# Moving a matmul kernel's steady-state transposes off TensorE, onto ScalarE, GpSimd and VectorE

## The chip, the cores and the metric

One core of a Trainium2 chip. The metric is the device time of one execution in microseconds (us). All times below are medians of runs in the fast state; how a ratio is formed is said at the result.

## The reference

```python
def setup_inputs():
    batch, m, k, n = 16, 512, 1024, 768
    # x (16,512,1024), weight (1024,768), add_value (16,512,768): float32 normal; scale 0.1

def reference(x, weight, scale, add_value):
    return (scale * np.matmul(x, weight) + add_value).astype(np.float32)
```

The rows are cut into 64 tiles of 128. A tile needs 0.52 MB of x, 0.39 MB of added values and 0.39 MB of stores; with 3.15 MB of weights the kernel moves 87.03 MB.

## The kernel before

x is cast to bf16; two bf16 neighbours are then looked at as one fp32 word, so a 128x1024 tile turns as four 128x128 blocks of words. Of every five tiles in the middle of the kernel, three are turned by TensorE (into PSUM, the memory that it writes, and moved from there to SBUF, the memory that it reads, by ScalarE: the evacuation) and two by VectorE, in sixteen block transposes a pair. All transfers are issued by SyncE, strictly in the order of `STREAM`; x has 16 slots, the added values and outputs share 32 slots.

```python
STREAM = [   # (what, first tile, tiles): the order in which SyncE issues transfers
    ("x", 0, 3), ("w", 0, 2), ("w", 2, 2), ("w", 4, 2), ("x", 3, 1), ("w", 6, 2),
    ("a", 0, 3), ("x", 4, 4), ("a", 3, 5), ("x", 8, 4), ("x", 12, 4), ("a", 8, 8),
    ("x", 16, 8), ("a", 16, 8), ("x", 24, 8), ("a", 24, 8), ("o", 0, 8), ("x", 32, 8),
    # ... cut ...
    ("o", 48, 8), ("o", 56, 4), ("o", 60, 3), ("o", 63, 1),
]
PAIRS = [14, 19, 24, 29, 34, 39, 44, 49, 54, 59]     # tiles t0 and t0+1, turned by VectorE

def cast_pair(t0):                                   # vx has one buffer
    for i in range(2):
        nc.gpsimd.tensor_copy(vx[:, i, :], xs[:, (t0 + i) % X_SLOTS, :])
def turn_pair(t0, a):                                # called in four successive steps
    for b in range(0, P, 32):
        nc.vector.transpose(
            vt[b:b + 32, :, 32 * a:32 * a + 32], pairs[32 * a:32 * a + 32, :, b:b + 32])
def transpose(t, pieces=1):
    # ... cut: cast_to(t); pairs = the cast tile as fp32 words ...
    for c in range(KC):
        nc.tensor.transpose(tp[:, c, :], pairs[:, c * P:(c + 1) * P], identity)
    # ... cut: ScalarE copies tp into xt ...
def step():
    for j in range(KJ):                              # 8 x (512 + 256 columns)
        if j == KJ // 2:
            if t + 1 not in in_pair: transpose(t + 1)
            cast_to(min(t + AHEAD, done["x"] - 1))   # AHEAD = 6
            if t + 7 in PAIRS: cast_pair(t + 7)
        product(t, j, BOTH)
    finish(t, BOTH[0], 0, N)                         # VectorE: ao = scale * mm + ao
    for a in range(4):
        if t + 6 - a in PAIRS: turn_pair(t + 6 - a, a)
```

## Time and profile before

| | before |
|---|---|
| time, median of 3 | 210.93 us (210.76 to 211.62) |
| span of the profiled run | 209.1 us |
| TensorE busy | 193.2 us, 92% |
| VectorE, ScalarE, GpSimd busy | 138.2, 47.2, 63.3 us |
| DMA | 87.03 MB, 97.7% of the 16 engines' span |

The prediction shows the lines. Two columns of the view by stretches: the DMA share (the mean busy share of the 16 DMA engines; 1.00 means that they were busy all the time, and in short stretches the view can read a little more) and the GB/s beside it.

### The profile page before, as it was taken

The page shows a single profiled execution, that of the slowest core. Times are in us where ns is not written, and L with a number is a line of the kernel's source. Part 1 is how long each engine was busy: PE and PEld are TensorE (multiplying, and loading weights), DVE is VectorE, ACT ScalarE, POOL GpSimd, SP SyncE. Part 2 cuts the span into 40 slices and gives each one's busy share as a digit, 9 for nine tenths or more (in the row PEclk, how much of TensorE's full clock was granted, in tenths as well). Part 3 has the DMA queues.
Part 4 walks back from the last instruction along what each step waited for, and adds up shares of the span by engine and source line. Part 5 has one row for each costly group of instructions (what it writes and reads, how often), then busy time and mean ns, then how long its engine had stood idle before and what let it go on. Part 6 is the DMA issues. An engine that isn't in the chain of part 4 may idle for free.

```text
span 209.1 us, 2949 instructions
## 1 busy us (share of the span) xinstructions
PE 193.2 (92%) x1187; PEld 117.9 (56%) x1210; DVE 138.2 (66%) x239; ACT 47.2 (23%) x50; POOL 63.3 (30%) x69
## 2 busy tenths in 40 slices
PE   7599499999899999999999999998999999999980
PEld 2355265665566566665666665564665656666640
DVE  0535533219969959999686986839994996973330
ACT  2523123323112113023031121130130230310210
POOL 1310524820292090502902707202703029200000
PEclk9889999999999999999999999999999999999998
DMA  6999999999999999999999999999999999999984
GB/s 235 418 425 444 424 422 429 450 450 407 423 456 417 418 437 395 458 439 422 431 429 425 440 428 423 437 429 423 428 432 432 458 404 423 432 440 432 407 378 179
DMA packets 4909, 87.21 MB, mean 417 GB/s; under 512 B 544, under 2 KB 544, under 8 KB 1312
## 3 DMA queue, kind: packets, MB, share of 16 engines
q1 hardware_dynamic: 4896, 87.03, 97.7%
q8 instruction: 9, 0.15, 0.3%
q14 instruction: 4, 0.03, 0.0%
HBM read 61.87 MB, written 25.17 MB: 416 GB/s over the span
## 4 chain that ended last, share of the span: by engine, by line
DMA 56%; PE 27%; DVE 8%; POOL 3%; issue 1%; SPq 0%; POOLq 0%; DVEq 0%
DMA xs<-in_x_dram 28%; PE mm L167 25%; DMA out_dram<-ao 16%; DMA ao<-in_add_value_dram 8%; DVE vt L119 5%; DMA ao<-in_weight_dram 4%; POOL vx L108 3%; PE tp L145 3%; DVE ao L175 2%; POOL xb L135 1%; SPq L101 0%; SPq L247 0%; POOLq L108 0%; POOLq L135 0%; DVEq L175 0%
## 5 line engine op out<-in xcount | busy, mean ns | idle before, releaser
L167 PE MATMUL mm<-w_bf,xt 128*128 128x512 bf16 (+1 forms) x687 | 122.1, 327 | 1.5 <-DVE ao L203 0.4
L167 PEld LDWEIGHTS <-xt 128*128 128x128 bf16 x704 | 66.0, 98 | 48.1 <-ACT xt L151 10.9
L175 DVE SCALAR_TENSOR_TENSOR ao<-mm,ao 128x768 f32<-128x768 f32 (+2 forms) x62 | 58.2, 944 | 43.9 <-PE mm L167 24.4
L151 ACT COPY xt<-tp 128x1024 bf16<-128x1024 bf16 (+1 forms) x47 | 44.6, 959 | 147.2 <-PE tp L145 147.2
L119 DVE STREAM_TRANSPOSE vt<-vx 32x256 f32<-32x256 f32 x160 | 69.7, 435 | 8.4 <-POOL vx L108 6.0
L135 POOL CAST xb<-xs 128x1024 bf16<-128x1024 f32 x41 | 41.3, 1042 | 55.7 <-DMA xs<-in_x_dram 55.7
L167 PE MATMUL mm<-w_bf,vt 128*128 128x256 bf16 (+1 forms) x314 | 54.6, 325 | 1.7 <-DVE vt L119 1.4
L167 PEld LDWEIGHTS <-vt 128*128 128x128 bf16 x320 | 31.1, 98 | 21.4 <-DVE vt L119 2.1
L108 POOL CAST vx<-xs 128x1024 bf16<-128x1024 f32 x20 | 20.3, 1042 | 53.7 <-DVE vt L119 43.3
L145 PE MATMUL tp<-identity,xb 128*128 128x128 f32 x176 | 27.1, 277 | 5.4 <-POOL xb L135 3.0
L145 PEld LDWEIGHTS tp<-identity,xb 128*128 128x128 f32 x176 | 20.7, 142 | 11.8 <-POOL xb L135 3.4
L103 DVE CAST w_bf<-ao 128x768 bf16<-128x768 f32 x8 | 4.1, 556 | 3.9 <-DMA ao<-in_weight_dram 3.9
L131 DVE CAST xb<-xs 128x512 bf16<-128x512 f32 x3 | 1.9, 697 | 5.8 <-DMA xs<-in_x_dram 5.8
L93 PE MATMUL warm<-zeros 128*128 128x512 bf16 x10 | 4.4, 631 | 1.2 <-DVE zeros L81 1.2
L203 DVE TENSOR_SCALAR ao<-mm 128x768 f32<-128x768 f32 x2 | 1.8, 953 | 2.4 <-PE mm L167 2.4
L133 POOL CAST xb<-xs 128x512 bf16<-128x512 f32 x2 | 1.6, 836 | 5.7 <-DMA xs<-in_x_dram 5.7
L93 PEld LDWEIGHTS <-zeros 128*128 128x128 bf16 x10 | 1.3, 142 | 3.4 <-issue 2.2
L234 DVE TENSOR_TENSOR ao<-ao 128x768 f32<-128x768 f32 x3 | 2.7, 950 | 0.0
L133 ACT CAST xb<-xs 128x512 bf16<-128x512 f32 x1 | 0.6, 618 | 5.0 <-DMA xs<-in_x_dram 5.0
L133 ACT ACT_TABLE_LOAD x1 | 1.3, 1283 | 0.7 <-PEq L277 0.7
L81 DVE MEMSET zeros<- 128x256 uint32 x1 | 0.3, 272 | 0.9 <-PEq L277 0.9
L200 ACT ACTIVATE ao<-mm 128x768 f32<-128x768 f32 x1 | 0.8, 817 | 0.0
(6 smaller groups left out, 0.9 us busy)
## 6 DMA issues: line engine op xcount, KB each, us to landing
xs<-in_x_dram SPq DMA_DIRECT2D x6, 4096.0 KB, 27.1
ao<-in_add_value_dram SPq DMA_DIRECT2D x7, 3072.0 KB, 24.2
out_dram<-ao SPq DMA_DIRECT2D x7, 3072.0 KB, 31.2
xs<-in_x_dram SPq DMA_DIRECT2D x3, 2048.0 KB, 25.2
ao<-in_weight_dram SPq DMA_DIRECT2D x4, 768.0 KB, 9.8
ao<-in_add_value_dram SPq DMA_DIRECT2D x1, 1920.0 KB, 21.1
xs<-in_x_dram SPq DMA_DIRECT2D x1, 1536.0 KB, 6.2
out_dram<-ao SPq DMA_DIRECT2D x1, 1536.0 KB, 12.3
```

The source lines that it names most:

```text
L93: nc.tensor.matmul(warm[:, 0:CUT], zeros[:, 0:P], zeros, start=True, stop=True)
L103: nc.vector.tensor_copy(w_bf[:, j + i, :], ao[:, s + i, :])
L108: nc.gpsimd.tensor_copy(vx[:, i, :], xs[:, (t0 + i) % X_SLOTS, :])
L119: nc.vector.transpose(vt[b:b + 32, :, 32 * a:32 * a + 32], pairs[32 * a:32 * a + 32, :, b:b + 32])
L131: nc.vector.tensor_copy(xb[:, 0:K // 2], src[:, 0:K // 2])
L133: other(xb[:, K // 2:K], src[:, K // 2:K])
L135: nc.gpsimd.tensor_copy(xb, src)
L145: nc.tensor.transpose(tp[:, c, :], pairs[:, c * P:(c + 1) * P], identity)
L151: nc.scalar.copy(dst[:, c:c + q, :, :], src[:, c:c + q, :, :])
L167: nc.tensor.matmul(mm_tiles[t, cols[0]][:, n0:n1], lhs(t, j), w_bf[:, j, n0:n1], start=(j == 0), stop=(j == KJ - 1))
L175: nc.vector.scalar_tensor_tensor(a, mm_tiles[t, part][:, n0:n1], float(scale), a, op0=mybir.AluOpType.mult, op1=mybir.AluOpType.add)
L234: nc.vector.tensor_add(ao[:, t, :], ao[:, EARLY_AT + t, :], ao[:, t, :])
```

## The change

Its intent is to take the transposes of tiles 14 to 59 off TensorE. A pair of tiles is cast and at the same time moved between 32-partition quadrants by ScalarE or GpSimd (alternately), 16 small copies a pair; one VectorE transpose then turns all 32x32 blocks. The order of transfers is redone for it: x comes earlier, added values later, and the last stores are smaller. The warm-up matmuls go, and the PSUM evacuation of tiles 4 to 13 moves from ScalarE to VectorE.

```diff
-    ("a", 0, 3), ("x", 4, 4), ("a", 3, 5), ("x", 8, 4), ("x", 12, 4), ("a", 8, 8),
-    ("x", 16, 8), ("a", 16, 8), ("x", 24, 8), ("a", 24, 8), ("o", 0, 8), ("x", 32, 8),
-    ...
-    ("o", 48, 8), ("o", 56, 4), ("o", 60, 3), ("o", 63, 1),
+    ("a", 0, 3), ("x", 4, 4), ("a", 3, 1), ("a", 4, 4), ("x", 8, 4), ("x", 12, 4),
+    ("x", 16, 4), ("a", 8, 8), ("x", 20, 4), ("x", 24, 8), ("o", 0, 8), ("a", 16, 8),
+    ("x", 32, 8), ("a", 24, 8), ("a", 32, 8), ("x", 40, 8), ("o", 8, 8), ("x", 48, 8),
+    ("a", 40, 8), ("o", 16, 8), ("x", 56, 8), ("a", 48, 8), ("o", 24, 8), ("o", 32, 8),
+    ("a", 56, 8), ("o", 40, 8), ("o", 48, 8), ("o", 56, 4), ("o", 60, 1), ("o", 61, 1),
+    ("o", 62, 1), ("l", 63, 1), ("r", 63, 1),          # left and right part of tile 63
-PAIRS = [14, 19, 24, 29, 34, 39, 44, 49, 54, 59]
+MOVED_ACT = [14, 18, 22, 26, 30, 34, 38, 42, 46, 50, 54, 58]
+MOVED_POOL = [16, 20, 24, 28, 32, 36, 40, 44, 48, 52, 56]
-AHEAD = 6
+AHEAD = 4
-    for _ in range(WARM):                              # ten warm-up matmuls
-        nc.tensor.matmul(warm[:, 0:CUT], zeros[:, 0:P], zeros, start=True, stop=True)
+    def move_pair(t0, a):                              # steps t0-8 to t0-5, a = 0..3
+        for b in range(4):
+            move = nc.scalar.copy if act else nc.gpsimd.tensor_copy
+            move(moved[t0][32 * b:32 * b + 32, :, a, :], src[32 * a:32 * a + 32, :, b, :])
+    def turn_moved(t0):                                # step t0-4, after its final add
+        nc.vector.transpose(
+            xt.rearrange("p i c m -> p (i c m)"),
+            moved.pop(t0).bitcast(fp32).rearrange("p c a k -> p (c a k)"))
     (cut: pools, the layout of xt, the loops that call these)
+        evacuate = nc.scalar.copy if t <= EARLY or t > LAST_PAIR else nc.vector.tensor_copy
```

## The prediction

> **What bounds the kernel now.** I read the page first: engine shares, slices, queue shares, chain.
>
> ```profile
> span 209.1 us, 2949 instructions
> PE 193.2 (92%) x1187; PEld 117.9 (56%) x1210; DVE 138.2 (66%) x239; ACT 47.2 (23%) x50; POOL 63.3 (30%) x69
> DMA  6999999999999999999999999999999999999984
> q1 hardware_dynamic: 4896, 87.03, 97.7%
> DMA 56%; PE 27%; DVE 8%; POOL 3%; issue 1%; SPq 0%; POOLq 0%; DVEq 0%
> ```
>
> Two things look full: TensorE (92%) and the DMA engines (97.7%). The reader should see that the row of DMA digits has no hole. Then I asked for busy time by stretch, to see how full the DMA really is:
>
> ```profile
> 0.00:5.00 5.00, 3.81 (x9) 1.34 (x10) 0.27 (x1) 1.28 (x1) 0.70 (x6) 1.00 0.67 231
> 5.00:200.00 195.00, 186.46 (x1162) 115.03 (x1184) 135.85 (x235) 45.85 (x49) 62.62 (x63) 0.99 1.00 429
> 200.00:205.00 5.00, 2.94 (x18) 1.49 (x16) 2.08 (x3) 0.11 (x1) 0.00 (x0) 1.00 0.90 377
> 205.00:210.00 5.00, 0.00 (x0) 0.00 (x0) 0.00 (x0) 0.00 (x0) 0.00 (x0) 0.70 0.24 95
> ```
>
> The last two columns are DMA share and GB/s. For 195 us the share is 1.00 and the rate 429 GB/s: the queue is never empty. The chain of waits ends differently, and this is the trap:
>
> ```profile
> 199.00 3.95 PE mm L167 x24
> 202.95 0.02 issue
> 202.97 0.42 DVE ao L175
> ```
>
> From 145 us to 203 us the chain is nearly pure TensorE. So the last product is TensorE's doing; but is the end? The issuing queue shows the last two stores issued from 201.33, the second at 203.4. The store issued at 201.33 took 5.9 us to land (207.2) and the last, 384 KB, 4.7 us (208.1). At 429 GB/s the last needs only 0.9 us of transfer: it stood behind a backlog. TensorE finished about as the DMA ran dry, not long after. Both limits meet at the end, and the DMA is the stiffer one.
>
> The groups that the change touches:
>
> ```profile
> L119 DVE STREAM_TRANSPOSE vt<-vx 32x256 f32<-32x256 f32 x160 | 69.7, 435 | 8.4 <-POOL vx L108 6.0
> L151 ACT COPY xt<-tp 128x1024 bf16<-128x1024 bf16 x41 | 41.5, 1012 | 146.3 <-PE tp L145 146.3
> L145 PE MATMUL tp<-identity,xb 128*128 128x128 f32 x176 | 27.1, 277 | 5.4 <-POOL xb L135 3.0 <-DVE xb L131 1.9 <-ACT xt L151 0.5
> L135 POOL CAST xb<-xs x41: 1042/1042/1043, 13.9 to 178.0; 128x1024 bf16<-128x1024 f32 x41
> L133 POOL CAST xb<-xs x2: 806/836/865, 7.0 to 7.8; 128x512 bf16<-128x512 f32 x2
> L133 ACT CAST xb<-xs x1: 618/618/618, 7.0 to 7.0; 128x512 bf16<-128x512 f32 x1
> ```
>
> In each, the columns after the bar are busy us and mean ns; the last three give minimum/median/maximum ns.
>
> **What the Trainium skill says.** "DMA: Bandwidth & Descriptors", Specifications, gives a fabric ceiling of 435 GB/s; the trace's 429 agrees, so I expect no more from scheduling. "VectorE: DVE Perf Modes", The three transpose paths, says that VectorE turns 32x32 blocks only: that is why data has to be moved between quadrants. The trace's 435 ns for 256 elements per partition is 256/0.96 = 267 ns at its 0.96 GHz plus 168 ns. "ScalarE: Activation LUTs", What ACT_TABLE_LOAD costs, gives 186 ns + 0.833 ns per element: 612 ns for 512, against 618 ns in the trace. "GPSIMD Engine Reference", Specifications, says GpSimd's SBUF interface is shared with VectorE, with contention when a VectorE instruction uses a 2-port mode or two SBUF inputs. The trace agrees: beside VectorE's casts in the head 512 elements took 806 to 865 ns, while 1024 elements take 1042 ns, never over 1045, beside block transposes and final adds.
>
> **The change part by part.**
>
> *TensorE.* The chain near the end repeats "2.63 us of matmuls x16, 0.44 us of transposes x4": a tile costs 2.63 us, and 0.44 more if it is transposed on the array. Before, 44 of 64 tiles are (20 are in pairs); after, 12 + 11 = 23 pairs take 46 tiles and leave 18. Saved: 26 x 0.44 = 11.4 us of TensorE. The weight reads keep the same stride as the former pairs had, which cost the same per matmul (325 against 327 ns).
>
> *VectorE.* Out: 160 x 435 ns = 69.7 us. In: 23 transposes of 128 x 1024; by the fit above 1024/0.96 + 168 = 1235 ns each, 28 us. It also takes the PSUM evacuation of tiles 4 to 13 (10, about 1.2 us each at one element a cycle). Net about 30 us less, on an engine at 66%.
>
> *ScalarE.* Out: most 1.01 us evacuations. In: 12 pairs x 16 moves x 0.61 = 117 us; 9.8 us per pair, one pair every four tiles.
>
> *GpSimd.* Out: most casts. In: 11 pairs x 16 moves. From 1042 ns for 1024 at 0.833 ns per element the fixed part is 189 ns, so 616 ns for 512 elements; 9.9 us per pair. This is an estimate: no instruction on 32 partitions that crosses quadrants is in this trace.
>
> *DMA.* Bytes are the same, 87.03 MB. Only order and last pieces change.
>
> **DMA ledger.** What counts is whether a load is issued before the queue runs dry. I take: queue drained at 2.4 us + MB/0.4283 per us (from the stretches above, 0.4283 being a slightly lower rate), landing 1.2 us later. On the old order it gives 7.3, 9.1, 10.9, 12.8, 14.0, 15.8 and 23.5 us for the first x, the weights with the next x tile, and tiles 4 to 7; consumers in the trace start at 6.98, 8.83, 10.70, 12.61, 13.90, 15.76, 23.48. Good enough. In the new order:
> - x 24..31 needs pair 14 moved: its data lands at 37.9, moves end near 47.7. The queue drains at 53.8: 6 us to spare.
> - x 32..39 needs pair 22, third in a row on ScalarE: 37.9 + 3 x 9.9 = 67.5; queue until 78.3: 11 spare.
> - x 40..47 needs pair 30, which waits for a buffer that the turn of pair 22 frees (about 83.5) and ends at 93.5; queue until 102.8: 9 spare.
> - x 48..55 needs pair 38, near 113.6; queue until 119.9: 6 spare.
> - x 56..63 needs pair 46, near 133.4; queue until 144.4: 11 spare.
>
> So no hole in the DMA, if a move takes under about 0.73 us. (Seven ScalarE pairs from 37.9 to 119.9 allow 82/112 us a move.)
>
> The new order delays the added values: a 8..15 lands at 50.1 (45.2 in the old order), a 16..23 at 79.5 (was 62.4). Tile 16's final add, due near 68, waits for it; with three PSUM buffers TensorE stops before tile 19 and resumes near 80.5. Then 45 tiles x 2.63 + 4 x 0.44 = 120.1 gives 200.6, plus some 1.7 us if the idle stretch halves the clock for 3.4 us as in the head (the stretch 5 to 15 us has mean clock 0.83, so 10 x 0.17 = 1.7 lost): about 202. So the 11.4 us saved are mostly spent waiting for loads.
>
> The last store drains at 2.4 + 87.03/0.4283 = 205.6, lands at 206.8; plus 1.0 us from landing to span's end (209.1 - 208.1), plus 1.8 us from span to measured time (210.93 - 209.1): 209.6. The old kernel's ledger gives the same 209.6, though it took 210.9: it lost 1.3 us in the tail (377 GB/s in the last full stretch). The new tail has even smaller pieces, but TensorE a little ahead. I keep half: 210.1.
>
> **Rivals.**
> 1. *TensorE sets the time.* For: 92% busy, and the chain from 145 to 203 us. Then removing 11.4 us gives about 200. Against: DMA share 1.00 for 195 us; 87.03 MB at 435 GB/s alone are 200.1 us before head, landing and launch. I give it almost nothing.
> 2. *GpSimd's moves are slow.* For: untested shape; the 836 ns casts. At 836 ns a pair takes 13.4 us, 11 pairs 147 us from tile 16's landing at 42.8: with some 4 us of casts the last ends at 194, then 8 tiles x 2.63 + 1.8 and the stores: about 223. Against: that value came beside VectorE casts, which the steady state no longer has.
> 3. *A hole in the queue.* Only 6 us to spare twice; moves of 0.78 us would empty it for some 5 us: 215.
> 4. *TensorE's tail*, if another wait for added values is longer than reckoned: 1 to 3 us, 211 to 213.
>
> **Range and chances.** The ledger's floor is 209.6, and at 435 GB/s 206.4; faster by 2% (under 206.7) needs that ceiling throughout. Slower (over 215.1) needs rival 2 or a bad rival 3. I predict 210.1, range 208.4 to 214.0; faster 0.05, same 0.81, slower 0.14.
>
> **What would show it.** Right: DMA share still 1.00 between 5 and 200 us near 429 GB/s; TensorE busy down by about 11 us or more (the ten warm-up matmuls go too) with a new idle stretch of some 10 us before 81 us, released by the adds that wait for a 16..23; moves of about 610 ns on both engines; transposes of about 1235 ns; ScalarE over 110 us busy. Wrong: moves over 0.73 us, the x loads in the queue's waits held by them past the drain times above, digits below 9 in the DMA row; or a DMA rate well off 429.

## The result and the profile after

The changed kernel takes 210.01 us (median of 4; 209.95 to 210.28) against 210.98 us of the kernel before in the same rounds. The ratio is 0.9952, interval [0.9928, 0.9975]; a ratio is the mean time of one kernel's fast runs over that of the other's of the same rounds, so it is not quite the ratio of the medians. By the threshold of 2% that the prediction uses, that is "same". 210.1 had been predicted.

The page of the changed kernel: span, busy times, the rows of TensorE, clock and DMA in 40 slices, and the chain of waits by engine.

```profile
span 208.5 us, 2886 instructions
PE 181.6 (87%) x1096; PEld 110.7 (53%) x1096; DVE 101.3 (49%) x111; ACT 129.0 (62%) x206; POOL 124.3 (60%) x199
PE   0599399980899997999999999999999999989960
PEclk9999889996589999999999999999999999999997
DMA  6999999999999999999999999999999999999995
DMA 75%; ACT 9%; PE 7%; DVE 3%; SPq 1%; issue 1%; DVEq 0%
```

TensorE lost 11.6 us of busy time, VectorE 37 us; ScalarE gained 82 us, GpSimd 61 us. The DMA row kept its nines, and the chain of waits, which used to end in 58 us of TensorE, is now 75% DMA and ends in 15 us of TensorE.

The groups of the new instructions (busy us, mean ns, then the idle time before them):

```profile
L118 ACT CAST va<-xs 32x512 bf16<-32x512 f32 x192 | 118.2, 616 | 28.8 <-DMA xs<-in_x_dram 19.1
L118 POOL CAST va<-xs 32x512 bf16<-32x512 f32 x176 | 106.8, 607 | 15.9 <-DVE xt L126 6.2
L126 DVE STREAM_TRANSPOSE xt<-va 128x1024 f32<-128x1024 f32 x23 | 28.4, 1234 | 0.0
L164 DVE COPY xt<-tp 128x1024 bf16<-128x1024 bf16 x10 | 6.9, 686 | 10.1 <-PE tp L156 10.1
```

The stretches that answer to those of before, and two in the middle (the last three columns are granted TensorE clock, DMA share and GB/s):

```profile
5.00:200.00 195.00, 180.04 (x1086) 109.79 (x1087) 100.14 (x109) 127.77 (x205) 123.61 (x193) 0.96 1.01 429
45.00:50.00 5.00, 1.38 (x9) 0.60 (x7) 0.00 (x0) 4.89 (x9) 4.66 (x8) 0.86 0.96 413
50.00:55.00 5.00, 2.06 (x7) 1.04 (x8) 2.42 (x3) 4.91 (x9) 4.65 (x9) 0.50 1.01 428
200.00:205.00 5.00, 1.58 (x12) 0.88 (x9) 1.12 (x2) 0.00 (x0) 0.00 (x0) 1.00 0.98 402
```

The reader should see that TensorE is idle from 46.4 to 53.0 us and has half its clock for some us afterwards (0.62 from 55 to 60 us), while the DMA moves 413 and 428 GB/s as if nothing had happened. The timeline shows what it waited for:

```profile
51.33 0.96 DVE L185 SCALAR_TENSOR_TENSOR ao<-mm,ao 128x768 f32<-128x768 f32 x1 [8.56 <-DMA ao<-in_add_value_dram]
52.21 0.68 DVE L164 COPY xt<-tp 128x1024 bf16<-128x1024 bf16 x1
52.95 2.74 PE L177 MATMUL mm<-w_bf,xt 128*128 128x512 bf16 x8 [6.57 <-DVE xt L164]
```

Tile 8's final add waits 8.56 us for its added values; the evacuation of tile 10 stands behind it in VectorE's order; TensorE waits for that evacuation.

**The landings, as a ledger.** The trace also has the time at which each transfer had landed. In a full queue an x block of 4.19 MB lands 9.70 us after the transfer before it, a block of adds or a store of 3.15 MB after 7.28 us: both are 432.3 GB/s. So every trace splits into an offset, 87.03 MB / 0.4323 = 201.3 us, and what the landings lost against that rate:

| run | offset | lost | last landing |
|---|---|---|---|
| before | 3.3 | 3.5 | 208.1 |
| before, second trace (experiment e9) | 3.1 | 3.8 | 208.2 |
| changed | 3.2 | 3.1 | 207.6 |
| changed, second trace (e10) | 3.2 | 2.9 | 207.4 |

Some 1.2 to 1.6 us of every loss are at the same place, the x block of tiles 8 to 11. Both traces of the kernel before lose another 0.8 and 1.2 us at the store of tiles 40 to 47 (landing at 193.6); neither trace of the changed kernel does. The store had been issued over 35 us earlier, so it was not a hole in the queue. That is about the size of the whole gain; why the loss is there is not shown. The traces hold one lead: they also list transfers of another kind, "instruction" (queues q8 and q14), nine of 16 KB in the kernel before and eight in the changed one. In these four traces each of the 13 landings that lost over 0.11 us overlaps one of them, and at the store of tiles 40 to 47 it starts at 187.2 us both times. But 37 other landings overlap one and lost no more than 0.11 us, and in experiment e5 an x block lost 0.73 us without one, so this is no more than a lead.

### The profile page after: what moved, and what is told of

Read it like the earlier page. It is cut to its first block, busy times and chain, and to the rows that moved or that the text cites. A ratio compares the mean times of both kernels' runs of the same rounds, so it can differ in the third digit from the quotient of the medians.

```text
span 208.5 us, 2886 instructions
## 1 busy us (share of the span) xinstructions
PE 181.6 (87%) x1096; PEld 110.7 (53%) x1096; DVE 101.3 (49%) x111; ACT 129.0 (62%) x206; POOL 124.3 (60%) x199
## 3 DMA queue, kind: packets, MB, share of 16 engines
q1 hardware_dynamic: 5616, 87.03, 98.2%
## 4 chain that ended last, share of the span: by engine, by line
DMA 75%; ACT 9%; PE 7%; DVE 3%; SPq 1%; issue 1%; DVEq 0%
DMA out_dram<-ao 35%; DMA ao<-in_add_value_dram 22%; DMA xs<-in_x_dram 13%; ACT va L118 9%; PE mm L177 6%; DMA ao<-in_weight_dram 5%; DVE ao L185 2%; DVE xt L126 1%; PE tp L156 1%; SPq L258 1%; SPq L99 0%; SPq L264 0%; SPq L272 0%; DVEq L185 0%
## 5 line engine op out<-in xcount | busy, mean ns | idle before, releaser
L177 PE MATMUL mm<-w_bf,xt 128*128 128x256 bf16 (+1 forms) x1024 | 173.8, 331 | 8.8 <-DVE xt L164 6.6
L177 PEld LDWEIGHTS <-xt 128*128 128x128 bf16 x1024 | 101.3, 99 | 76.9 <-DVE xt L164 7.0
L118 ACT CAST va<-xs 32x512 bf16<-32x512 f32 x192 | 118.2, 616 | 28.8 <-DMA xs<-in_x_dram 19.1
L118 POOL CAST va<-xs 32x512 bf16<-32x512 f32 x176 | 106.8, 607 | 15.9 <-DVE xt L126 6.2
L146 POOL CAST xb<-xs 128x1024 bf16<-128x1024 f32 x15 | 15.2, 1040 | 43.4 <-PE tp L156 22.5
L164 ACT COPY xt<-tp 128x512 bf16<-128x512 bf16 (+1 forms) x11 | 8.2, 785 | 35.3 <-PE tp L156 35.3
L126 DVE STREAM_TRANSPOSE xt<-va 128x1024 f32<-128x1024 f32 x23 | 28.4, 1234 | 0.0
L156 PE MATMUL tp<-identity,xb 128*128 128x128 f32 x72 | 12.9, 314 | 11.2 <-DVE xb L142 7.4
L156 PEld LDWEIGHTS tp<-identity,xb 128*128 128x128 f32 x72 | 9.8, 161 | 13.7 <-issue 7.6
L164 DVE COPY xt<-tp 128x1024 bf16<-128x1024 bf16 x10 | 6.9, 686 | 10.1 <-PE tp L156 10.1
```

The lines of the kernel that those rows point to most:

```text
L118: move(moved[t0][32 * b:32 * b + 32, :, a, :], src[32 * a:32 * a + 32, :, b, :])
L126: nc.vector.transpose(xt.rearrange("p i c m -> p (i c m)"), moved.pop(t0).bitcast(fp32).rearrange("p c a k -> p (c a k)"))
L146: nc.gpsimd.tensor_copy(xb, src)
L164: evacuate(xt_tiles[t][:, c:c + q, :].bitcast(bf16), tp[:, c:c + q, :].bitcast(bf16))
L177: nc.tensor.matmul(mm_tiles[t, cols[0]][:, n0:n1], lhs(t, j), w_bf[:, j, n0:n1], start=(j == 0), stop=(j == KJ - 1))
```

## The experiments

All give right results unless it is said otherwise. "Before" is the kernel before on the same chip in the same rounds.

### Each half alone: e1 and e2

e1 is the kernel before with only the new order of transfers and the split last stores; e2 is the changed kernel with the old order.

```diff
 e1: kernel before
-STREAM = [ ...old... ]
+STREAM = [ ...new... ]
-            nc.sync.dma_start(rows(out_v, s, n), ao[:, k:k + n, :])
+            n0, n1 = {"o": (0, N), "l": (0, CUT), "r": (CUT, N)}[op]
+            nc.sync.dma_start(rows(out_v, s, n)[:, :, n0:n1], ao[:, k:k + n, n0:n1])
 e2: changed kernel
-STREAM = [ ...new... ]
+STREAM = [ ...old... ]
```

> The kernel before, with only the new order of transfers (and the split last stores). Queue theory (the DMA bytes set the time, and TensorE is only just quick enough): the late adds stop TensorE near tile 11 as they do in the changed kernel, but here it still has the slow array transposes to do, so it ends near 208 us and the time rises to 212 to 215. Rival, order theory (the small gain of the change comes from the order and the finer tail alone): 209.5 to 210.5.

Measured: 221.63 us, ratio 1.0506 [1.0478, 1.0533]. Slower by more than either theory said. The queue's own timeline (start, us, what) and the stretch of the hole:

```profile
100.97 0.43 SPq L262 DMA_DIRECT2D out_dram<-ao  x1
127.79 0.33 SPq L248 DMA_DIRECT2D xs<-in_x_dram  x1
```

```profile
122.00:132.00 10.00, 10.00 (x65) 6.03 (x63) 7.57 (x15) 2.02 (x2) 4.98 (x5) 1.00 0.38 136
```

The store issued at 100.97 had landed at 123.7; the next load, x 48, was asked for only at 127.8, so the share fell to 0.38. It waited for GpSimd's cast of the last pair in those slots, and in that trace GpSimd's pair casts sat 82.8 us behind VectorE's turns (one buffer), which themselves stand behind final adds that wait for TensorE. So the old preparation cannot run ahead of TensorE; the landings lost 14.6 us. The order theory is refuted: the order alone, with the finer tail, is a loss.

> The changed kernel with the old order of transfers. Queue theory: DMA share still 1.00, 209.5 to 212; the loads of x come too late for TensorE to use its freedom. Rival, TensorE theory (the array transposes were the cost, and the late adds ate what was saved): no stop of 7 us near tile 11, so 200 to 205.

Measured: 217.85 us (five fast runs; a sixth, 220.01, was slow), ratio 1.0342 [1.0302, 1.0382]. Here the hole is at the end. Three lines of the timeline of ScalarE and VectorE and one stretch:

```profile
174.32 10.02 ACT L117 CAST va<-xs 32x512 bf16<-32x512 f32 x16 [15.19 <-DMA xs<-in_x_dram]
```

```profile
171.04 0.96 DVE L184 SCALAR_TENSOR_TENSOR ao<-mm,ao 128x768 f32<-128x768 f32 x1 [0.60 <-PE mm L176]
184.75 1.25 DVE L125 STREAM_TRANSPOSE xt<-va 128x1024 f32<-128x1024 f32 x1 [12.76 <-POOL va L117]
```

```profile
205.00:212.00 7.00, 6.50 (x42) 3.78 (x40) 3.03 (x4) 1.62 (x2) 0.00 (x0) 1.00 0.24 100
```

The last x block lands at 174.2 in the old order; a pair takes 10 us to move, VectorE stands still for 12.8 us, and TensorE is still multiplying at 211 when the queue has long run dry (share 0.24). TensorE theory (200 to 205) is refuted; the queue theory was right in kind, x came too late, but I had underrated it by 6 us. The two halves of the change need each other.

### Relieve the queue: e3, e4 and e8

To see what the change is worth without the queue, e3 (kernel before), e4 (changed kernel) and e8 (changed kernel with earlier adds) store only two tiles of every eight. Their outputs are wrong, which doesn't matter for the times.

```diff
 e3
-            nc.sync.dma_start(rows(out_v, s, n), ao[:, k:k + n, :])
+            nc.sync.dma_start(rows(out_v, s, n if n < 8 else 2), ao[:, k:k + (n if n < 8 else 2), :])
 e4, e8
+            n = 2 if n == 8 else n
             nc.sync.dma_start(rows(out_v, s, n)[:, :, n0:n1], ao[:, k:k + n, n0:n1])
```

> The kernel before, storing only 2 of every 8 tiles of the seven large stores (wrong result on purpose): 16.5 MB less, 38.5 us of transfer. Queue theory: the queue no longer binds (floor about 171); TensorE, whose 187 us of products and transposes start in earnest near 25 us, binds at 204 to 206. A theory in which the queue alone matters says 172 to 180.

> The changed kernel with the same cut of the stores (wrong result on purpose). Queue theory: with the queue relieved, the transposes taken off the array show: 198 to 201, some 5 us under the kernel before with the same cut, where with full stores it was 1. If the moves or another wait had replaced the transposes, no gap between the two.

Measured: e3 208.56 us, ratio 0.9894 [0.9875, 0.9913]; e4 204.67 us, ratio 0.9704 [0.9687, 0.9721]. The last 75 us before 200, e3 first:

```profile
125.00:200.00 75.00, 74.83 (x479) 46.07 (x477) 53.75 (x95) 16.19 (x16) 19.97 (x20) 1.00 0.64 256
```

```profile
125.00:200.00 75.00, 74.43 (x464) 45.08 (x462) 39.33 (x40) 42.91 (x68) 39.25 (x62) 1.00 0.70 272
```

The queue is relieved there (shares 0.64 and 0.70; before 125 us they are still 0.96 and 0.97) and TensorE is full in both. So these times are what TensorE and the stores behind its last product allow: 208.6 for the kernel before, 204.7 for the changed one. Two things follow. The change is worth 3.9 us there (208.56 - 204.67), and 1.0 us with the full stores: most of it is hidden under the queue. And before the change the two limits stood only 2.3 us apart (210.9 and 208.6). The 3.9 us are not the transposes alone. TensorE's last product was added at 202.9 in e3 and at 199.9 in e4, 3.0 us apart; the rest is the smaller last stores (the last one landed 3.1 us after that add in e3, 1.9 us in e4). The order of transfers and the warm-up differ too; no run takes only the transposes off. Both runs came out above what I expected, by 2.6 and 3.7 us over the upper ends, TensorE's end being later than I had reckoned. In e4 the stop near 50 us is there as before (the final add of tile 7 at 40.3, of tile 8 at 51.5), so 204.7 does not show all that TensorE could gain.

> The same early adds with only 2 of every 8 tiles stored (wrong result on purpose). Queue theory: now neither the queue nor the stop holds TensorE: 193 to 197, 8 us or more under the kernel before with that cut.

Measured: 202.76 us, ratio 0.9602 [0.9581, 0.9622]; a miss by 6 us, though lower than e4. The stop did not go, it changed its cause. VectorE's timeline:

```profile
49.44 0.96 DVE L185 SCALAR_TENSOR_TENSOR ao<-mm,ao 128x768 f32<-128x768 f32 x1 [0.61 <-PE mm L177]
56.53 1.25 DVE L126 STREAM_TRANSPOSE xt<-va 128x1024 f32<-128x1024 f32 x1 [6.13 <-ACT va L118]
57.70 0.65 DVE L164 COPY xt<-tp 128x1024 bf16<-128x1024 bf16 x1
```

With the adds first, x 12 lands at 46.5 in place of 39.2, so pair 14 is moved later; VectorE waits 6.13 us for it before its turn, and the evacuation that TensorE needs stands behind that turn. e8 is 5.8 us under e3, not 8.

### Take the stop away: e5

```diff
-("x", 8, 4), ("x", 12, 4), ("x", 16, 4), ("a", 8, 8), ("x", 20, 4), ("x", 24, 8), ("o", 0, 8), ("a", 16, 8),
+("x", 8, 4), ("a", 8, 8), ("x", 12, 4), ("x", 16, 4), ("x", 20, 4), ("a", 16, 8), ("x", 24, 8), ("o", 0, 8),
```

> The changed kernel with the added values of tiles 8 to 15 and 16 to 23 asked for earlier (before x 12 and before x 24). Queue theory: the stop of TensorE near tile 11 goes, and the clock drop with it; TensorE ends near 197 in place of 201.6, and the time stays at 209.3 to 210.3. Rival, stall theory (the 7 us stop and the half clock after it ate the gain): 200 to 204.

Measured: 211.24 us, ratio 1.0010 [0.9994, 1.0027]. The stall theory (200 to 204) is not borne out, but the experiment did not remove what it was to remove: as in e8 the stop only moved (VectorE waited 5.98 us for pair 14, until 56.3). TensorE's last product ended later, not earlier (last final add at 204.7 in place of 201.6), because of one more stop, at the added values of tiles 48 to 55, which landed at 164.9:

```profile
164.97 0.96 DVE L185 SCALAR_TENSOR_TENSOR ao<-mm,ao 128x768 f32<-128x768 f32 x1 [8.90 <-DMA ao<-in_add_value_dram]
```

```profile
165.98 9.28 PE L177 MATMUL mm<-w_bf,xt 128*128 128x512 bf16 x38 [3.10 <-DVE ao L185]
```

The granted clock was 0.52 from 165 to 170 us. The time did not follow TensorE's end, 3.1 us later: it rose by some 1.2 us against the changed kernel, of which the landings account for 1.1 (they lost 4.2 us, 3.1 there). Full freedom of TensorE from its stops stays untried.

### How much room the moves have: e6, e7 and e11

Useless copies after every four moves, from a weight tile into a scratch tile: 256 elements on ScalarE (e6), twice 512 on ScalarE (e7), 512 on GpSimd (e11).

```diff
+        if act:                                   # e11: if not act, nc.gpsimd.tensor_copy, 512
+            nc.scalar.copy(dummy[:, 0:256], w_bf[:, 0, 0:256])   # e7: 0:512, twice
         if a == 3:
             cast_pairs.add(t0)
```

> The changed kernel with one useless copy of 256 elements (about 0.39 us) on ScalarE after every four moves: a move costs 0.71 us in effect, just under the ledger's limit of 0.73. Queue theory: x 48 is asked for about when the queue runs dry, 210 to 211. If ScalarE's moves already bind the kernel, each of 48 copies shows: 210 + 48 x 0.39 = 229.

Measured: 213.96 us, ratio 1.0141 [1.0124, 1.0159]. The copies took 405 ns each, 0.72 us a move in effect. The queue's timeline:

```profile
120.59 0.33 SPq L261 DMA_DIRECT2D xs<-in_x_dram  x1
122.04 0.33 SPq L267 DMA_DIRECT2D ao<-in_add_value_dram  x1
```

x 48 was asked for at 120.6, when the last transfer in the queue was about to land (122.0). The landings lost 1.1 us at x 48 and 2.2 us at the adds after it. So at 0.72 the hole is already there: 19.4 us of useless work cost 4 us.

> Two useless copies of 512 elements (1.2 us) after every four moves: 0.92 us a move in effect. Ledger: a pair takes 14.7 us, 12 pairs from 39 us end at 215; tiles 58 to 63 and the stores follow: 235 to 240, with holes in the DMA row, and the x loads held by ScalarE in the queue's waits. A theory in which the moves have far more room says under 215.

Measured: 246.03 us, ratio 1.1673 [1.1649, 1.1697]. SyncE waited 134.9 us for ScalarE's moves before x loads (90.1 in the changed kernel), and the landings lost 39.8 us. Holes as the ledger has them, and 6 us more than it said: each copy took 618 ns, so a pair cost 15.1 us (the distance of two x loads, 30.3 us, halved), not 14.7.

> One useless copy of 512 elements (about 0.6 us) on GpSimd after every four of its moves: 0.76 us a move in effect. Ledger: a GpSimd pair takes 12.1 us; pair 36 is moved near 119 and pair 44 near 143, both about 2 us before the queue runs dry, so small holes at most: 210 to 213. Rival 2 of the prediction as it was put (GpSimd's slowness reaches the end of the kernel directly) says 11 pairs x 2.4 us = 26 us more, 236.

Measured: 218.67 us, ratio 1.0379 [1.0351, 1.0406]. Neither: more than the small holes, far less than 26 us. The copies took 610 ns. x 48 was asked for at 123.2, after the queue had run dry (122.2), and one wait shows the second path:

```profile
DVE xt L129 <- POOL va L119: 34.3, 7, 7.2
```

VectorE waited 34.3 us in seven turns for GpSimd's moves; its final adds, and through its turns ScalarE's buffers (17.1 us of waiting), stood behind it. With 8.5 us more than the changed kernel's 210.12 in the same rounds, at 0.76 us a move, GpSimd too has little room in the changed kernel.

### The noise, and once more: e9 and e10

Unchanged copies of the two kernels.

> The kernel before against itself, for the noise: ratio within 0.998 to 1.002. Its trace tells whether the 0.8 us that the DMA lost at the store of tiles 40 to 47 (landing 193.6) belongs to the kernel or to that run: if to the kernel, the loss is there again.

> The changed kernel once more, with more rounds: ratio 0.993 to 0.998, so that a gain of some 0.5% is clear of the noise of the run before it. In its trace the landings lose 2.5 to 3.5 us against 432 GB/s in all, as in the first trace (3.1).

Measured: e9 ratio 1.0001 [0.9989, 1.0013]; e10 210.12 us, ratio 0.9967 [0.9955, 0.9979]. The changed kernel's gain, 0.3 to 0.5%, is outside the noise of the kernel before against itself. The landings of both traces are in the table above: the loss at the store of tiles 40 to 47 came back (1.23 us).

### An attempt to beat both: e12

```diff
-            nc.sync.dma_start(ao[:, s:s + 2, :], w_v[:, j // 2, :, :])
+            nc.scalar.dma_start(ao[:, s:s + 2, :], w_v[:, j // 2, :, :])
```

> The changed kernel with the four weight loads issued from ScalarE's queue while SyncE issues the x loads, an attempt to beat both kernels. The DMA share is 0.75 and 0.57 in the second and third us of the kernel before; if that is the issuing of one queue, up to 0.7 us is to be had: 209.3 to 209.8. If it is the first transfer's own start, 209.9 to 210.3.

Measured: 226.05 us, ratio 1.0720 [1.0696, 1.0744]. The attempt failed for a reason of mine. ScalarE's sequencer in the head:

```profile
6.79 0.62 ACT L144 CAST xb<-xs 128x512 bf16<-128x512 f32 x1 [4.78 <-DMA xs<-in_x_dram]
10.78 0.90 ACTq L99 DMA_DIRECT2D ao<-in_weight_dram  x2
```

The weight loads come after the first tiles' cast and copies in ScalarE's program order, so they were asked for at 10.8 us in place of 1.2. What the first two microseconds could give is still open. No version here beat the changed kernel.

## Why the prediction was right, and where not

**The bound.** Right: DMA share 1.01 and 429 GB/s from 5 to 200 us, as forecast, and e4 against the changed kernel shows 5.3 us of difference from cut stores alone. "I give it almost nothing" was too strong for TensorE: e3 puts its limit at 208.6, only 2.3 us under the measured time.

**TensorE.** 11.6 us less busy time, predicted "about 11 us or more". But the warm-up matmuls alone were 4.4 us, so with the 11.4 us of transposes some 15.8 were due; part of the difference was taken back by matmuls at a lower clock (0.69 from 25 to 30 us, 0.50 and 0.62 from 50 to 60).

**Durations.** Moves 616 and 607 ns (predicted 610 and 616), block transpose 1234 ns (1235). The rate of 0.833 ns an element used for GpSimd stood in no trace; 1040 ns for 1024 elements and 607 for 512 give 0.85, close enough. VectorE's evacuation was the one mis-sized term: 686 ns, not 1.2 us; it cost nothing.

**The ledger.** The five x loads were issued at 49.2, 71.3, 96.0, 116.1 and 136.2 us; it had 47.7, 67.5, 93.5, 113.6 and 133.4. The queue never ran dry. Its limit of "about 0.73 us" a move was too high: e6 lost 4 us at 0.72, e11 8.5 us at 0.76. A load needs time between its issue and its bytes: in e1 x 48, issued into an empty queue, landed after 12.2 us where the transfer itself takes 9.7 (12.2 and 12.1 us in e6 and e11). The ledger had no such term of 2.5 us before a transfer, and it left out VectorE's waits. Why the blocks behind such a late load lose time as well (2.2 us in e6) is not shown.

**The stop.** Predicted before tile 19, near 80 us, for the adds of tile 16. It came before tile 10, at 46 us, for the adds of tile 8, 6.6 us long with the clock at 0.50 after it; at 80 us it was 1.2 us. I had the landing of a 8..15 (50.1 predicted, 51.2 measured) in hand and did not follow it. e1 tells the causes apart: with the same order of transfers, the same landing (51.4) and the evacuation still on ScalarE, TensorE stopped too, before tile 11, for 4.5 us, waiting for a final add to free a PSUM buffer:

```profile
52.47 2.72 PE L168 MATMUL mm<-w_bf,xt 128*128 128x512 bf16 x8 [4.48 <-DVE ao L176]
```

So most of the stop is the late adds, a wait that the prediction reckoned for tile 16 but not for tile 8. That it came a tile earlier and was 2.1 us longer in the changed kernel fits VectorE's order, though the two kernels differ in more than that. TensorE's end (predicted 202, measured near 201.6) came out right all the same, since the wait that it did forecast still set the place from which TensorE ran on: the adds of tile 16 landed at 80.8 (79.5 predicted), TensorE went on at 81.9 (80.5), and from there it waited only once more, 0.6 us for the adds of tiles 56 to 63. The 1.7 us put down for a lower clock there did not come (1.00 from 80 to 85 us), which made up for the later start.

**The tail.** "It lost 1.3 us in the tail (377 GB/s in the last full stretch)" was the wrong place. From the landing of the store of tiles 48 to 55 to the last one the kernel before took 7.3 us, the changed one 7.5. The largest difference lies at the store of tiles 40 to 47. The rate was 432.3, not 428.3, with losses of about 3 us in lumps; the two errors largely cancel in the sum (201.3 + 3.1 = 204.4 against 203.2), and the half microsecond kept for a tail loss that was not there covers part of the rest. So the 210.1 rests partly on luck in its last microsecond.

## What to carry to other kernels

When the DMA share stands at 1.00, count bytes over rate before anything else: work removed from a full compute engine shows only down to that floor. Here the change gave 1.0 us, which is not even shown to be TensorE's, and 3.9 with the queue relieved. Ask for each load early by more than the arithmetic says (2.5 us here). Follow every late transfer to the engine that waits for it, and count the order within an engine as a dependency: here an evacuation stood behind an add that waited for memory, and TensorE behind both. An order of transfers and the engines that free its buffers are one design; here each half alone cost 3 to 5%.

## What the Trainium skill lacked or had wrong

- "GPSIMD Engine Reference", Cross-partition — where GPSIMD wins, says that the other compute engines' datapaths work in lockstep at the same offset on all partitions. ScalarE moved 32 partitions to another quadrant while casting in 616 ns for 512 elements, against 618 ns for 512 elements that stay where they are; GpSimd took 607 ns. No page has the cost of such moves on ScalarE or GpSimd.
- "VectorE: DVE Perf Modes", Rules for kernel authors, says of elementwise work on a matmul's output to accept 1x (PSUM source); it does not say that 16-bit data can do better. The bf16 copy of 1024 elements from PSUM took 686 ns, less than the 1067 ns that 1024 elements at one per 0.96 GHz cycle need. The tier table of the same page (up to 2x from PSUM) agrees with the run; the prediction's "one element a cycle" is the rule's figure, and was too slow.
